# Two steps in turn at each change of resident operands in an encoder layer's projections

## The chip, the cores and the metric

The kernel runs on one core of a Trainium2 chip. Time is device time of the whole program in microseconds (us); lower is better. Before the change it takes 2800.76 us, the median of three runs (2798.44 to 2802.41).

## The reference, cut to what matters

One encoder layer for two requests of 2048 and 1024 tokens (3072 tokens, width 1024), in float32:

```python
z = rmsnorm(x) @ w_in
f = fft2(z[..., :512]).real
zs = gelu(z[..., 512:])
u, v = zs[..., :512], rmsnorm(zs[..., 512:])
g = u * (einsum('hpq,bnqhc->bnphc', w_spatial, v) + b)
x = x + rmsnorm(concat([f, g]) @ w_out)
a = conv3(rmsnorm(x) @ w_up)
gate, up = a[..., :2816], a[..., 2816:]
y = x + rmsnorm((gelu(gate) * up) @ w_down)
...
```

## The kernel before, in words

Each large product, the gating heads' `zs`, the up projection and the down projection, is done by Strassen's scheme: a product of two 2x2 block matrices takes seven block products, numbered B11, B21, T4, T2, T3, T1, B22 (0 to 6), and sums of their results. Each operand is split in two rounded parts, a high part (a cast on ScalarE, L100 and L154) and the rest (a subtraction on VectorE or GpSimd, L101 and L156), and three matmuls replace one. A block product with an inner size of 512 is thus 12 matmuls of 128x512 into one of 8 PSUM banks (`Step.mm`, L200). I call such a block product a **product**, and the seven of one output tile pair a **step**.

A **stage** (`Stage`) keeps one side resident in SBUF: seven operands of four pieces (28 tiles named `sox`, `sow` or `sog`, each made by one ScalarE cast and one subtraction: pieces 0 and 2 on VectorE, 1 and 3 on GpSimd; in the first up block B11 and T2 are all VectorE's). Steps stream past it with their own small operands (`w0u` to `w6u`, names ending in u for up, d for down, g for the gating heads).

The order is: 24 Fourier products in two halves with the 12 gating steps between; 12 mixing steps; three blocks of the up projection (`Up`, three resident sets of tokens, 22 steps each, 7 products of 12 matmuls); three parts of the down projection (`Down`, three resident sets of weights, 12 steps each, the first with 9 matmuls a product). So operands that are resident change five times, twice in `Up`, on entering `Down`, twice in `Down`; the gating heads and the first up block begin with none.

The order of the instructions is written out by hand. `at(slot, order, fn)` puts work into numbered slots; one slot holds one product of TensorE, and within it loads come first, then preparation (PREP), matmuls (MM), what is done with the result (OUT), stores. Each engine runs its instructions in that order and waits by semaphores. SyncE issues all DMAs, in order. A step that begins in slot s prepares `w` of a product two slots ahead (`Step.prep`), then reads the result (`post`): Up keeps four results in PSUM, lets ScalarE scale them (`centre`) and VectorE add the convolution's two other taps to each (`taps`, L1146), and GpSimd multiplies the gate in (`Up.gate`, L1183). In the first up block and in `Down` and the heads, GpSimd also makes four sums of the streamed operand (`Step.sums`, L179 to L182); w4u's subtraction is GpSimd's (`POOL = (4,)`).

At a change of operands `turnover` spreads the 28 pieces of the new stage over ten slots, from six before the first step of the new stage to four after, as the last old step and the first new one run. All large tiles come from one pool `U` of 43 buffers, half-size ones from `H`.

Of the kernel before, what the change touches and what calls it, by code (L numbers as in the profile page):

```python
# [33 lines left out]
def tile_trunk(  # L34
# [8 lines left out]
    H = ctx.enter_context(tc.tile_pool(name="h", bufs=12))  # L43
# [528 lines left out]
    for j, s in ((T4, 9), (T2, 10), (T3, 11), (T1, 12), (B22, 13)):  # L572
        at(s, PREP + 0.6, heads.prep, j)
# [4 lines left out]
    for pr in range(12):  # L578
        s = SB + 7 * pr
        g = Gate(heads, pr)  # L580
        steps(s, g)
# [4 lines left out]
        at(s + 1, OUT + 0.2, g.vout, 0)
        at(s + 5, OUT + 0.2, g.vout, 1)
        at(s + 7, OUT + 0.6, g.vscale)
        at(s + 6, OUT + 0.3, g.uout, 1)
        at(s + 7, OUT + 0.3, g.uout, 0)  # L590
        at(s + 8, OUT + 0.5, g.vnorm, 0)
        at(s + 8, OUT + 0.5, g.vnorm, 1)
        at(s + 10, PREP + 0.5, g.vsplit)
        at(s + 13, MM + 0.5, g.spatial)
        at(s + 13, OUT + 0.5, g.gate)
        at(s + 15, MM + 0.5, g.turn)
        at(s + 15, OUT + 0.5, g.turned)
        at(s + 16, STORE, g.gstore)
# [598 lines left out]
    for blk in range(3):  # L1197
# [5 lines left out]
        if blk:  # L1203
            turnover(s, stage, Up.ORDER)
        else:
            for i, j in enumerate(Up.ORDER):
# [39 lines left out]
    class Down(Step):  # L1246
# [15 lines left out]
        def cstore(self):  # L1262
            for i in range(2):
                for h in range(2):
                    nc.sync.dma_start(c_d[2 * self.tp + i, :, h], self.quads(i)[h])
# [88 lines left out]
    for q in range(3):  # L1354
# [13 lines left out]
        turnover(s, stage)  # L1368
        if q == 2:
            at(s - 2, LOAD, po_load)  # L1370
        for tp in range(12):
            d = Down(stage, q, tp)
            steps(s, d)
            if q == 0:
                at(s + 8, STORE, d.cstore)
                s += 7
                continue
            at(s if d.closing else s + 3, LOAD, d.cload)
            if not d.closing:
                at(s + 6, OUT + 0.2, d.cadd, 1)  # L1380
                at(s + 7, OUT + 0.2, d.cadd, 0)
            if q == 1:
                at(s + 8, STORE, d.cstore2, 1)
                at(s + 9, STORE, d.cstore2, 0)
            elif tp == 11:
                at(s + 1, LOAD, d.closing_load)
                at(s + 2, OUT + 0.1, d.square, 0, 0)
                at(s + 4, OUT + 0.1, d.square, 1, 0)
                at(s + 5, OUT + 0.1, d.square, 1, 1)
                at(s + 6, OUT + 0.1, d.square, 0, 1)  # L1390
                at(s + 6, OUT + 0.2, d.closing_out)
            else:
                e = 3 if d.closing else 0
                at(s + 10 - e, MM, d.squares)
                at(s + 11 - e, LOAD, d.xload)
                at(s + 11 - e, PREP + 0.5, d.scale)
                at(s + 12 - e, PREP + 0.5, d.yout, 1)
                at(s + 14 - e, OUT + 0.3, d.yout, 0)
                at(s + 14 - e, STORE, d.ystore, 1)
# [123 lines left out]
```

## Time and profile before

| | |
|---|---|
| median of three runs | 2800.76 us |
| the profiled execution | 2798.38 us |
| its span on the core | 2796.6 us |
| TensorE busy | 2659.1 us (95%) |
| VectorE busy | 2218.6 us (79%) |
| GpSimd busy | 1361.6 us (49%) |
| ScalarE busy | 1192.7 us (43%) |
| mean clock granted to TensorE | 0.982 |

A busy TensorE is not a TensorE at its peak: matmuls overlap, and in steady steps of `Up` one starts every 0.227 us (19.04 us for the 84 of a step). What is lost is therefore read as the time of a step over 19.04 us, place by place, and the wait that ends last there says why.

### The profile page before, as it was taken

The page shows a single profiled execution, that of the slowest core. Times are in us where ns is not written, and L with a number is a line of the kernel's source. Part 1 is how long each engine was busy: PE and PEld are TensorE (multiplying, and loading weights), DVE is VectorE, ACT ScalarE, POOL GpSimd, SP SyncE. Part 2 cuts the span into 40 slices and gives each one's busy share as a digit, 9 for nine tenths or more (in the row PEclk, how much of TensorE's full clock was granted, in tenths as well). Part 3 has the DMA queues.
Part 4 walks back from the last instruction along what each step waited for, and adds up shares of the span by engine and source line. Part 5 has one row for each costly group of instructions (what it writes and reads, how often), then busy time and mean ns, then how long its engine had stood idle before and what let it go on. Part 6 is the DMA issues. An engine that isn't in the chain of part 4 may idle for free. (4 is left out here: it accounts for less than half of the span.)

```text
span 2796.6 us, 35290 instructions
## 1 busy us (share of the span) xinstructions
PE 2659.1 (95%) x11930; PEld 2173.2 (78%) x11930; DVE 2218.6 (79%) x3295; ACT 1192.7 (43%) x2273; POOL 1361.6 (49%) x867
## 2 busy tenths in 40 slices
PE   8899999998879999989999999999998999999997
PEld 7678887887758888877888877888886877887775
DVE  5788866767888787888777788888888677669998
ACT  5445534564634444454444444444443242214332
POOL 3856612547774656562212233212224347669787
PEclk9999999999989999999999999999999999999999
DMA  9446667567953545464343363334353465466665
GB/s 336 165 154 205 206 229 258 200 198 226 294 210 113 184 162 179 145 215 128 113 133 128 114 225 112 115 124 135 118 176 115 132 218 175 153 201 212 209 210 200
DMA packets 323926, 498.10 MB, mean 178 GB/s; under 512 B 27232, under 2 KB 176224, under 8 KB 323744
## 3 DMA queue, kind: packets, MB, share of 16 engines
q1 hardware_dynamic: 323744, 495.85, 53.7%
q8 instruction: 93, 1.52, 0.2%
q14 instruction: 89, 0.73, 0.1%
HBM read 337.42 MB, written 158.35 MB: 177 GB/s over the span
## 5 line engine op out<-in xcount | busy, mean ns | idle before, releaser
L1183 POOL TENSOR_TENSOR t0u<-t0u,t1u 128x1024 f32<-128x1024 f32 x66 | 184.2, 2791 | 237.3 <-issue 145.1
L101 POOL TENSOR_TENSOR w4u<-a4u,w4u 128x512 fp32r<-128x512 f32 x44 | 57.1, 1297 | 446.2 <-ACT w4u L100 401.9
L200 PE MATMUL p4u<-sox,w4u 128*128 128x512 f32 x792 | 199.3, 399 | 17.0 <-POOL w4u L101 12.2
L200 PE MATMUL p2u<-sox,w2u 128*128 128x512 f32 x792 | 196.6, 397 | 8.2 <-DVE w2u L101 8.2
L200 PE MATMUL p0u<-sox,w0u 128*128 128x512 f32 x792 | 194.1, 393 | 7.9 <-DVE w0u L101 4.8
L200 PE MATMUL p1u<-sox,w1u 128*128 128x512 f32 x792 | 194.3, 394 | 6.8 <-DVE w1u L101 6.8
L200 PE MATMUL p6u<-sox,w6u 128*128 128x512 f32 x792 | 192.8, 392 | 4.0 <-DVE w6u L101 4.0
L200 PEld LDWEIGHTS p4u<-sox,w4u 128*128 128x128 f32 x792 | 150.1, 192 | 56.2 <-POOL w4u L101 17.2
L200 PE MATMUL p3u<-sox,w3u 128*128 128x512 f32 x792 | 191.8, 390 | 1.7 <-DVE w3u L101 1.7
L200 PE MATMUL p5u<-sox,w5u 128*128 128x512 f32 x792 | 191.0, 390 | 1.0 <-DVE w5u L101 1.0
L1134 ACT ACTIVATE t1u<-p2u,cbt,cwt 128x512 f32<-128x512 f32 x66 | 51.4, 779 | 321.3 <-DVE p2u L1122 321.3
L200 PEld LDWEIGHTS p2u<-sox,w2u 128*128 128x128 f32 x792 | 151.3, 192 | 42.2 <-DVE w2u L101 10.5
L200 PEld LDWEIGHTS p0u<-sox,w0u 128*128 128x128 f32 x792 | 149.2, 189 | 42.4 <-DVE w0u L101 7.5
L200 PEld LDWEIGHTS p1u<-sox,w1u 128*128 128x128 f32 x792 | 150.8, 191 | 39.6 <-DVE w1u L101 8.1
L200 PEld LDWEIGHTS p6u<-sox,w6u 128*128 128x128 f32 x792 | 149.7, 189 | 37.0 <-DVE w6u L101 5.7
L200 PEld LDWEIGHTS p3u<-sox,w3u 128*128 128x128 f32 x792 | 148.1, 188 | 33.7 <-DVE w3u L101 3.0
L200 PEld LDWEIGHTS p5u<-sox,w5u 128*128 128x128 f32 x792 | 148.8, 188 | 32.9 <-DVE w5u L101 1.9
L208 ACT COPY ud<-p0d 128x512 f32<-128x512 f32 x34 | 20.0, 587 | 344.7 <-PE p0d L200 344.7
L1134 ACT ACTIVATE t0u<-p1u,cbt,cwt 128x512 f32<-128x512 f32 x66 | 51.4, 779 | 260.7 <-DVE p1u L1128 260.7
L1182 ACT ACTIVATE t0u<-t0u 128x1024 f32<-128x1024 f32 x66 | 70.1, 1062 | 155.4 <-DVE t0u L1146 114.4
L1146 DVE SCALAR_TENSOR_TENSOR t0u<-p6u,cwt,t0u 128x511 f32<-128x511 f32 (+4 forms) x220 | 111.6, 532 | 5.2
L1146 DVE SCALAR_TENSOR_TENSOR t1u<-p2u,cwt,t1u 128x511 f32<-128x511 f32 (+4 forms) x220 | 111.7, 533 | 3.1
(363 smaller groups left out, 7235.5 us busy)
## 6 DMA issues: line engine op xcount, KB each, us to landing
g_d<-t0u SPq DMA_DIRECT2D x66, 512.0 KB, 2.9
srx<-xo_d SPq DMA_DIRECT2D x42, 512.0 KB, 6.8
xT<-xT SPq DMA_DIRECT2D x24, 512.0 KB, 8.5
xc<-xc SPq DMA_DIRECT2D x24, 512.0 KB, 5.7
zz<-z_d SPq DMA_DIRECT2D x48, 256.0 KB, 5.5
xr<-x_po SPq DMA_DIRECT2D x24, 512.0 KB, 5.2
xo_d<-hT SPq DMA_DIRECT2D x48, 256.0 KB, 4.0
ra0d<-g_d SPq DMA_DIRECT2D x24, 512.0 KB, 6.8
```

What stands on the lines that cost most here:

```text
L101: (eng or vec).tensor_tensor(l, src, h.bitcast(F32), op=ALU.subtract)
L200: nc.tensor.matmul(ps, lhsT=w[:, a, k], rhs=op[k][:, b], start=k == 0 and a + b == 0, stop=k == n - 1 and a == 1)
L208: nc.scalar.copy(self.u, p[0])
L1134: nc.scalar.activation(t[:, i], p, AF.Identity, bias=cbt[:, ti : ti + 1], scale=cwt[:, ti, 1:2])
L1146: vec.scalar_tensor_tensor(d, a, w, d, op0=ALU.mult, op1=ALU.add)
L1182: nc.scalar.activation(ga, ga, AF.Gelu_apprx_tanh)
L1183: nc.gpsimd.tensor_tensor(ga, ga, self.t[1], op=ALU.mult)
```

## The change

The two last steps that use a stage and the two first that use the next are run in pairs, product by product: first B11 of the one, then B11 of the other, and so on over 14 slots (`place` and `pos` give a step its first slot and its stride). This is done for the first and last two steps of each up block, the first two of each down part, the last two of the first two parts, and the first two gating steps. `turnover` gets a lead of 12 slots and a span of 22. In the first up block and the heads an operand is prepared every second slot. The sums of paired down steps are made three slots later, `u.POOL` is empty for both of the first up steps, the taps of Up's first half stand at fixed distances from product 4, and `H` has 14 buffers. The loads and sums of the down weights (`wd_load`, `wd_sums`, `wd_store`) move eight slots back. Elsewhere a step of stride 1 keeps its places.

```diff
-    H = ctx.enter_context(tc.tile_pool(name="h", bufs=12))
+    H = ctx.enter_context(tc.tile_pool(name="h", bufs=14))
...
-    def steps(s, step, ahead=2):
-        at(s - 6, LOAD, step.load)
-        at(s - ahead, PREP - 0.2, step.sums)
-        products(s, step)
...
+    def place(s, step, which=None):
+
+        step.s0, step.by = (s, 1) if which is None else (s + which, 2)
+
+    def pos(step, k):
+        return step.s0 + min(k, 0) + step.by * min(max(k, 0), 6) + max(k - 6, 0)
+
+    def steps(step, ahead=2):
+        at(pos(step, -6), LOAD, step.load)
+        at(pos(step, -ahead), PREP - 0.2, step.sums)
+        products(step)
+
+    def products(step):
         for i, j in enumerate(step.ORDER):
-            at(s + i - 2, PREP, step.prep, j)
-            at(s + i, MM, step.mm, j)
-            at(s + i, OUT, step.post, j)
-
-    TURN = 10
-    def turnover(s, stage, order=tuple(range(7))):
+            at(pos(step, i) - 2, PREP, step.prep, j)
+            at(pos(step, i), MM, step.mm, j)
+            at(pos(step, i), OUT, step.post, j)
+
+    def turnover(s, stage, order=tuple(range(7)), lead=6, span=10):
 
         for n in range(28):
             j, k = order[n // 4], n % 4
-            d = s - 6 + n * TURN // 28
+            d = s - lead + n * span // 28
...
-    for j, s in ((T4, 9), (T2, 10), (T3, 11), (T1, 12), (B22, 13)):
+    for j, s in ((T4, 10), (T2, 12), (T3, 14), (T1, 16), (B22, 18)):
         at(s, PREP + 0.6, heads.prep, j)
...
-        steps(s, g)
+        place(*((SB, g, pr) if pr < 2 else (s, g)))
+        steps(g, 0 if pr < 2 else 2)
...
-        at(s + 8, OUT + 0.5, g.vnorm, 0)
-        at(s + 8, OUT + 0.5, g.vnorm, 1)
...
+        at(pos(g, 8), OUT + 0.5, g.vnorm, 0)
+        at(pos(g, 8), OUT + 0.5, g.vnorm, 1)
...
-            turnover(s, stage, Up.ORDER)
+            turnover(s, stage, Up.ORDER, 12, 22)
         else:
             for i, j in enumerate(Up.ORDER):
-                at(s + [-3, -3, -2, -2, -1, 0, 1][i], LOAD, stage.load, j)
-                at(s + [-2, -2, -1, 0, 1, 2, 3][i], PREP - 0.3, stage.prep, j)
+                d = s + max(2 * i - 3, -2)
+                at(d - 1 - (i > 0), LOAD, stage.load, j)
+                at(d, PREP - 0.3, stage.prep, j)
         for ft in range(NFT):
             u = Up(stage, blk, ft)
-            if ft == 0 and blk == 0:
+
+            pair = ft < 2 or ft > NFT - 3
+            place(s - 7 * (ft % 2) if pair else s, u, ft % 2 if pair else None)
+            first = blk == 0 and ft < 2
+            if first:
                 u.POOL = ()
-            if blk == 0 and ft < 2:
-                at(s - (2, 4)[ft], LOAD, u.load)
-                at(s - 2, PREP - 0.2, u.sums)
-                products(s, u)
+                at(u.s0 - 2, LOAD, u.load)
+                at(u.s0 - 2, PREP - 0.2, u.sums)
+                products(u)
...
-            at(s + 4, OUT + 0.1, u.centre, 1)
-            at(s + 5, OUT + 0.2, u.taps, 1, 0)
-            at(s + 6, OUT + 0.1, u.centre, 0)
-            at(s + 6, OUT + 0.2, u.taps, 1, 1)
-            at(s + 7, OUT + 0.2, u.taps, 0, 0)
-            at(s + 8, OUT + 0.6, u.taps, 0, 1)
...
+            at(pos(u, 4), OUT + 0.1, u.centre, 1)
+            at(pos(u, 4) + 1, OUT + 0.2, u.taps, 1, 0)
+            at(pos(u, 4) + 2, OUT + 0.2, u.taps, 1, 1)
+            at(pos(u, 6), OUT + 0.1, u.centre, 0)
+            at(pos(u, 7), OUT + 0.2, u.taps, 0, 0)
+            at(pos(u, 8), OUT + 0.6, u.taps, 0, 1)
...
-        turnover(s, stage)
+        turnover(s, stage, range(7), 12, 22)
...
             d = Down(stage, q, tp)
-            steps(s, d)
+            pair = tp < 2 or tp > 9 and q < 2
+            place(s - 7 * (tp % 2) if pair else s, d, tp % 2 if pair else None)
+            steps(d, -1 if pair else 2)
```

**TensorE, the last two steps of the second up block (`u1_20`, `u1_21`).** In names such as `p0u1_20`, 0 is the product, 1 the block counted from 0, 20 the step. Before, where the first of them ends and the second begins:

```order
L200 MATMUL p1u1_20_14463<-sox112_11143,w1u1_20_14408 128x512 x3
L200 MATMUL p1u1_20_14463<-sox113_11146,w1u1_20_14408 128x512 x3
L200 MATMUL p0u1_21_14493<-sox100_10844,w0u1_21_14434 128x512 x3
L200 MATMUL p0u1_21_14493<-sox101_10847,w0u1_21_14434 128x512 x3
L200 MATMUL p0u1_21_14493<-sox102_10850,w0u1_21_14434 128x512 x3
L200 MATMUL p0u1_21_14493<-sox103_10878,w0u1_21_14434 128x512 x3
L200 MATMUL p3u1_21_14528<-sox130_10881,w3u1_21_14460 128x512 x3
L200 MATMUL p3u1_21_14528<-sox131_10884,w3u1_21_14460 128x512 x3
```

After, at their first products:

```order
L200 MATMUL p0u1_20_14325<-sox100_10711,w0u1_20_14268 128x512 x3
L200 MATMUL p0u1_20_14325<-sox101_10714,w0u1_20_14268 128x512 x3
L200 MATMUL p0u1_20_14325<-sox102_10737,w0u1_20_14268 128x512 x3
L200 MATMUL p0u1_20_14325<-sox103_10760,w0u1_20_14268 128x512 x3
L200 MATMUL p0u1_21_14349<-sox100_10711,w0u1_21_14294 128x512 x3
L200 MATMUL p0u1_21_14349<-sox101_10714,w0u1_21_14294 128x512 x3
L200 MATMUL p0u1_21_14349<-sox102_10737,w0u1_21_14294 128x512 x3
L200 MATMUL p0u1_21_14349<-sox103_10760,w0u1_21_14294 128x512 x3
```

The two steps now read the same resident `sox10*` one right after the other. The last use of B11 (`sox10*`) thus stands twelve products ahead of the end of the stage, where before it stood six ahead.

**VectorE, the taps of the same steps.** Before, from the weight of the second step's first product on:

```order
L101 TENSOR_TENSOR w0u1_21_14434<-a0u1_21_14364,w0u1_21_14434 128x512
L1125 TENSOR_TENSOR p6u1_20_14437<-vu1_20_14358,p6u1_20_14437 128x512
L1146 SCALAR_TENSOR_TENSOR t1u1_20_14425<-p5u1_20_14389,cwt_82,t1u1_20_14425 128x511 x2
L1146 SCALAR_TENSOR_TENSOR t1u1_20_14425<-p5u1_20_14389,cwt_82,t1u1_20_14425 128x1
L1146 SCALAR_TENSOR_TENSOR t1u1_20_14425<-halo_99,cwt_82,t1u1_20_14425 128x1
L101 TENSOR_TENSOR w3u1_21_14460<-a3u1_21_14384,w3u1_21_14460 128x512
L1128 TENSOR_TENSOR p1u1_20_14463<-uu1_20_14334,p1u1_20_14463 128x512
L1146 SCALAR_TENSOR_TENSOR t1u1_20_14425<-p2u1_20_14411,cwt_82,t1u1_20_14425 128x511 x2
L1146 SCALAR_TENSOR_TENSOR t1u1_20_14425<-p2u1_20_14411,cwt_82,t1u1_20_14425 128x1
L1164 SCALAR_TENSOR_TENSOR fix_101<-p2u1_20_14411,cwt_82,part_100 128x1
L1146 SCALAR_TENSOR_TENSOR t0u1_20_14477<-p6u1_20_14437,cwt_82,t0u1_20_14477 128x511 x2
```

After, between products 4 and 6 of the pair (L1153 is the old L1146, L1132 the old L1125):

```order
L1153 SCALAR_TENSOR_TENSOR t1u1_20_14547<-p5u1_20_14485,cwt_82,t1u1_20_14547 128x511 x2
L1153 SCALAR_TENSOR_TENSOR t1u1_20_14547<-p5u1_20_14485,cwt_82,t1u1_20_14547 128x1
L1153 SCALAR_TENSOR_TENSOR t1u1_20_14547<-halo_99,cwt_82,t1u1_20_14547 128x1
L101 TENSOR_TENSOR w1u1_20_14586<-a1u1_20_14500,w1u1_20_14586 128x512
L1132 TENSOR_TENSOR p6u1_20_14592<-vu1_20_14394,p6u1_20_14592 128x512
L1153 SCALAR_TENSOR_TENSOR t1u1_20_14547<-p2u1_20_14533,cwt_82,t1u1_20_14547 128x511 x2
L1153 SCALAR_TENSOR_TENSOR t1u1_20_14547<-p2u1_20_14533,cwt_82,t1u1_20_14547 128x1
L1171 SCALAR_TENSOR_TENSOR fix_101<-p2u1_20_14533,cwt_82,part_100 128x1
L1153 SCALAR_TENSOR_TENSOR t1u1_21_14575<-p5u1_21_14508,cwt_82,t1u1_21_14575 128x511 x2
L1153 SCALAR_TENSOR_TENSOR t1u1_21_14575<-p5u1_21_14508,cwt_82,t1u1_21_14575 128x1
L1153 SCALAR_TENSOR_TENSOR t1u1_21_14575<-halo_99,cwt_82,t1u1_21_14575 128x1
L101 TENSOR_TENSOR w1u1_21_14618<-a1u1_21_14523,w1u1_21_14618 128x512
```

Before, a tap of one step stood between two weight subtractions (L101); now two taps, one of each step, stand there together.

**GpSimd, the first up block.** `s0u` to `s3u` are the sums of a step's streamed operand, es and ds the last mixing step's residual. Before, from the last resident pieces on:

```order
L156 TENSOR_TENSOR sox011_7316<-srx010_7241,sox011_7316 128x512
L156 TENSOR_TENSOR sox013_7322<-srx012_7243,sox013_7322 128x512
L179 TENSOR_TENSOR s0u0_1_7368<-ra1u0_1_7310 128x512
L180 TENSOR_TENSOR s1u0_1_7369<-s0u0_1_7368,ra0u0_1_7309 128x512
L181 TENSOR_TENSOR s2u0_1_7370<-ra0u0_1_7309,ra1u0_1_7310 128x512
L182 TENSOR_TENSOR s3u0_1_7371<-ra0u0_1_7309,s1u0_1_7369 128x512
L93 TENSOR_SCALAR r2111_v_7395<-ss2111_7343 128x2
L94 TENSOR_TENSOR r2111_y_7396<-r2111_v_7395,power_84 128x2
L898 TENSOR_TENSOR es111_7036<-es111_7036,xr1111_7045 128x1024
L898 TENSOR_TENSOR ds111_7100<-ds111_7100,xr1110_7043 128x1024
L101 TENSOR_TENSOR w4u0_1_7427<-s2u0_1_7370,w4u0_1_7427 128x512
```

After, from the sums of the first step on:

```order
L182 TENSOR_TENSOR s3u0_0_7128<-ra0u0_0_7109,s1u0_0_7126 128x512
L179 TENSOR_TENSOR s0u0_1_7158<-ra1u0_1_7143 128x512
L180 TENSOR_TENSOR s1u0_1_7159<-s0u0_1_7158,ra0u0_1_7142 128x512
L181 TENSOR_TENSOR s2u0_1_7160<-ra0u0_1_7142,ra1u0_1_7143 128x512
L182 TENSOR_TENSOR s3u0_1_7161<-ra0u0_1_7142,s1u0_1_7159 128x512
L156 TENSOR_TENSOR sox041_7224<-srx040_7138,sox041_7224 128x512
```

The second step's sums now stand ahead of the resident pieces, and its `w4u` is no longer on GpSimd.

## Rows read from the trace of the kernel before

**Rows 1.** The page: busy time of the engines, share of the span, instructions.
```profile
PE 2659.1 (95%) x11930; PEld 2173.2 (78%) x11930; DVE 2218.6 (79%) x3295; ACT 1192.7 (43%) x2273; POOL 1361.6 (49%) x867
```

**Rows 2.** Windows, TensorE's L200 alone: stretch, length, busy (matmuls), clock, DMA share, GB/s.
```profile
90.75:144.80 54.05, 44.48 (x169) 0.91 0.49 164
778.28:842.35 64.07, 46.84 (x169) 0.84 0.51 183
1215.97:1289.42 73.45, 64.33 (x254) 0.93 0.52 179
1651.17:1705.85 54.68, 43.84 (x170) 0.94 0.52 185
2086.65:2150.86 64.21, 54.59 (x211) 0.92 0.50 157
2279.38:2344.55 65.17, 57.35 (x233) 0.95 0.64 206
2515.91:2581.97 66.06, 59.94 (x254) 0.97 0.64 215
```

**Rows 3.** Windows, steady steps: length, then busy PE, PEld, DVE, ACT, POOL; clock.
```profile
1117.90:1196.79 78.89, 78.01 (x346) 63.62 (x345) 64.44 (x99) 35.94 (x69) 45.16 (x29) 1.00 0.48 156
1460.64:1536.80 76.16, 76.16 (x338) 63.09 (x337) 59.62 (x117) 32.17 (x52) 16.78 (x8) 1.00 0.38 125
1896.11:1972.27 76.16, 76.16 (x338) 63.06 (x337) 64.71 (x133) 32.18 (x52) 16.28 (x8) 1.00 0.39 124
2165.00:2222.12 57.12, 57.12 (x254) 47.30 (x253) 37.52 (x57) 13.92 (x32) 17.68 (x16) 1.00 0.42 129
2382.49:2458.65 76.16, 76.16 (x338) 63.08 (x337) 49.89 (x57) 16.91 (x32) 48.83 (x33) 1.00 0.52 166
2659.96:2740.01 80.05, 78.57 (x338) 62.22 (x337) 76.75 (x73) 26.70 (x48) 64.35 (x41) 1.00 0.67 211
```

**Rows 4.** Timeline, TensorE, second change of blocks: start, length, what, [idle before <-releaser].
```profile
1695.10 4.63 PE L200 MATMUL p2u<-sox,w2u 128*128 128x512 f32 x10 [3.28 <-DVE w2u L101]
```

**Rows 5.** Line L156 on VectorE: operand subtractions, ns min/median/max.
```profile
L156 DVE TENSOR_TENSOR sox<-srx,sox x46: 677/1177/2890, 768.6 to 1698.4; 128x512 fp32r<-128x512 f32 x46
L156 DVE TENSOR_TENSOR sow<-srw,sow x42: 677/1772/2894, 2093.0 to 2556.7; 128x512 fp32r<-128x512 f32 x42
```

**Rows 6.** Timeline, VectorE, the same change of blocks.
```profile
1652.40 0.69 DVE L1128 TENSOR_TENSOR p1u<-uu,p1u 128x512 f32<-128x512 f32 x1
1653.00 1.65 DVE L1146 SCALAR_TENSOR_TENSOR t1u<-p2u,cwt,t1u 128x511 f32<-128x511 f32 x3
...
1659.43 0.68 DVE L1112 TENSOR_TENSOR vu<-uu,p3u 128x512 f32<-128x512 f32 x1
...
1664.70 2.27 DVE L101 TENSOR_TENSOR w6u<-a6u,w6u 128x512 fp32r<-128x512 f32 x1
1666.90 3.47 DVE L156 TENSOR_TENSOR sox<-srx,sox 128x512 fp32r<-128x512 f32 x2
```

**Rows 7.** Timeline, GpSimd, the same change of blocks.
```profile
1657.20 6.43 POOL L156 TENSOR_TENSOR sox<-srx,sox 128x512 fp32r<-128x512 f32 x4 [0.75 <-ACT sox L154]
```

**Rows 8.** Window, VectorE's L156 alone, the same change: length, busy (pieces).
```profile
1640.00:1705.00 65.00, 15.95 (x14) 0.95 0.53 183
```

**Rows 9.** Waits of VectorE over five steps of the second block.
```profile
DVE w0u L101 <- ACT w0u L100: 10.4, 5, 2.1
```

**Rows 10.** Timeline, VectorE, start of the first block.
```profile
768.59 12.56 DVE L156 TENSOR_TENSOR sox<-srx,sox 128x512 fp32r<-128x512 f32 x8
```

**Rows 11.** Timeline, ScalarE, start of the first block.
```profile
777.61 0.62 ACT L100 CAST w0u<-ra0u 128x512 fp32r<-128x512 f32 x1 [7.68 <-DMA ra0u<-w_up]
```

**Rows 12.** Timeline, GpSimd, start of the first block.
```profile
825.65 1.71 POOL L101 TENSOR_TENSOR w4u<-s2u,w4u 128x512 fp32r<-128x512 f32 x1
```

**Rows 13.** Timeline, TensorE, start of the first block.
```profile
827.42 4.18 PE L200 MATMUL p4u<-sox,w4u 128*128 128x512 f32 x10 [7.75 <-POOL w4u L101]
```

**Rows 14.** Timeline, VectorE, gating head of the first step.
```profile
127.36 5.88 DVE L442 SCALAR_TENSOR_TENSOR v2g<-v2g,rvg_y,gsg 128x128 f32<-128x128 f32 x8
```

More of the change, by code (lines that the diff above doesn't have):

```diff
@@ L585, in tile_trunk @@
             at(s - 2, OUT + 0.5, stats[pr].root)
[L586 to L590, printed above, removed]
-        at(s + 8, OUT + 0.5, g.vnorm, 0)
-        at(s + 8, OUT + 0.5, g.vnorm, 1)
[L593 to L598, printed above, removed]
+        at(pos(g, 1), OUT + 0.2, g.vout, 0)
+        at(pos(g, 5), OUT + 0.2, g.vout, 1)
+        at(pos(g, 7), OUT + 0.6, g.vscale)
+        at(pos(g, 6), OUT + 0.3, g.uout, 1)
+        at(pos(g, 7), OUT + 0.3, g.uout, 0)
+        at(pos(g, 8), OUT + 0.5, g.vnorm, 0)
+        at(pos(g, 8), OUT + 0.5, g.vnorm, 1)
+        at(pos(g, 10), PREP + 0.5, g.vsplit)
+        at(pos(g, 13), MM + 0.5, g.spatial)
+        at(pos(g, 13), OUT + 0.5, g.gate)
+        at(pos(g, 15), MM + 0.5, g.turn)
+        at(pos(g, 15), OUT + 0.5, g.turned)
+        at(pos(g, 16), STORE, g.gstore)
     gpm = None
@@ L688, in tile_trunk @@
     for i in range(NFT // 2):
-        at(SB + 7 * i + 1, LOAD, wd_load, i)
-        at(SB + 7 * i + 3, PREP, wd_sums, i)
-        at(SB + 7 * i + 7, STORE, wd_store, i)
+        at(SB + 7 * i + 9, LOAD, wd_load, i)
+        at(SB + 7 * i + 11, PREP, wd_sums, i)
+        at(SB + 7 * i + 15, STORE, wd_store, i)
     class Side:
@@ L1260, in fetch, with cstore @@
                 )
[L1262 to L1265, printed above, removed]
+        def cstore(self, i, h):
+            nc.sync.dma_start(c_d[2 * self.tp + i, :, h], getattr(self, f"c{i + 1}{h + 1}"))
         def cload(self):
@@ L1372, in tile_trunk @@
             d = Down(stage, q, tp)
-            steps(s, d)
+            pair = tp < 2 or tp > 9 and q < 2
+            place(s - 7 * (tp % 2) if pair else s, d, tp % 2 if pair else None)
+            steps(d, -1 if pair else 2)
+            s += 7
             if q == 0:
-                at(s + 8, STORE, d.cstore)
-                s += 7
+                at(pos(d, 2), STORE, d.cstore, 0, 0)
+                at(pos(d, 6), STORE, d.cstore, 1, 0)
+                at(pos(d, 6), STORE, d.cstore, 1, 1)
+                at(pos(d, 7), STORE, d.cstore, 0, 1)
@@ L1377, in tile_trunk @@
                 continue
-            at(s if d.closing else s + 3, LOAD, d.cload)
+            at(pos(d, 0 if d.closing else 3), LOAD, d.cload)
             if not d.closing:
-                at(s + 6, OUT + 0.2, d.cadd, 1)
-                at(s + 7, OUT + 0.2, d.cadd, 0)
+                at(pos(d, 6), OUT + 0.2, d.cadd, 1)
+                at(pos(d, 7), OUT + 0.2, d.cadd, 0)
             if q == 1:
-                at(s + 8, STORE, d.cstore2, 1)
-                at(s + 9, STORE, d.cstore2, 0)
+                at(pos(d, 8), STORE, d.cstore2, 1)
+                at(pos(d, 9), STORE, d.cstore2, 0)
@@ L1385, in tile_trunk @@
             elif tp == 11:
[L1386 to L1391, printed above, removed]
+                at(pos(d, 1), LOAD, d.closing_load)
+                at(pos(d, 2), OUT + 0.1, d.square, 0, 0)
+                at(pos(d, 4), OUT + 0.1, d.square, 1, 0)
@@ L1392, in tile_trunk @@
+                at(pos(d, 5), OUT + 0.1, d.square, 1, 1)
+                at(pos(d, 6), OUT + 0.1, d.square, 0, 1)
+                at(pos(d, 6), OUT + 0.2, d.closing_out)
             else:
                 e = 3 if d.closing else 0
[L1394 to L1399, printed above, removed]
@@ L1400, in tile_trunk @@
-                at(s + 15 - e, STORE, d.ystore, 0)
-            s += 7
+                at(pos(d, 10 - e), MM, d.squares)
+                at(pos(d, 11 - e), LOAD, d.xload)
+                at(pos(d, 11 - e), PREP + 0.5, d.scale)
+                at(pos(d, 12 - e), PREP + 0.5, d.yout, 1)
+                at(pos(d, 14 - e), OUT + 0.3, d.yout, 0)
+                at(pos(d, 14 - e), STORE, d.ystore, 1)
+                at(pos(d, 15 - e), STORE, d.ystore, 0)
     with tc.manual_schedule():
```

13 lines of the change are left out of this document (6 added, 7 removed).

## The prediction

> **What bounds the kernel now.** The page first: TensorE is busy 95% of the span, VectorE 79% [rows 1], but that share counts matmuls that overlap. So I took places one by one, in windows of TensorE's L200 alone [rows 2], against steady steps [rows 3]. A steady step of the second up block takes 76.16/4 = 19.04 us, one of the first down part 57.12/4 = 14.28. What the seven places of the change lose against that:
>
> - first two gating steps: 54.05 - 38.08 = 16.0, of which the first mixing products of the heads, also TensorE work, are a part (about 1.5, an estimate): 14.5
> - first two up steps: 64.07 - 38.08 = 26.0
> - up block 0 to 1: 73.45 - 57.12 = 16.3
> - up 1 to 2: 54.68 - 38.08 = 16.6
> - up to down: 64.21 - 19.04 - 28.56 = 16.6
> - down 0 to 1: 65.17 - 14.28 - 38.08 = 12.8
> - down 1 to 2: 66.06 - 57.12 = 8.9
>
> Together 111.7 us, 4% of the span. No change of order can give more.
>
> Which engine is late there? The timeline of up 1 to 2: a steady product takes 19.04/7 = 2.72 us, and in the change TensorE stops in the middle of products, waiting for a weight that VectorE has yet to subtract, 3.28 us in one case, after which ten matmuls alone took 4.63 [rows 4]; the mean clock granted over that window was 0.94 [rows 2]. VectorE is in order and full: besides its own work it makes 14 of the 28 pieces. Alone one takes 0.68 us (the least), but the median is 1.18 in up and 1.77 in down [rows 5]: it stretches while GpSimd makes the other pieces beside it. Two took 3.47 and a weight subtraction 2.27, while a sum that reads PSUM took 0.68 within GpSimd's four pieces [rows 6, 7]. So **VectorE bounds the changes, and GpSimd lengthens its work**. The 14 pieces took 15.95 us there [rows 8]; with the 2 x 1.6 by which two weights were stretched, about 19 us of extra VectorE work. Ten slots have about 2 us free for it and the weights stand about 1.5 us ahead: 19 - 2 - 1.5 = 15.5, near the 16.6 seen.
>
> **The change, part by part.**
>
> *More slots.* Free VectorE time per step is its idle time less one wait for ScalarE's cast behind `centre`, 10.4/5 = 2.1 us, which does not go away [rows 9]. From rows 3: second up block (76.16 - 59.62)/4 - 2.1 = 2.0; first (78.89 - 64.44)/4 - 2.1 = 1.5; third (76.16 - 64.71)/4 - 2.1 = 0.8; down 0, with about 1.5 kept for the like wait, 3.4; down 1, 5.1; down 2, whose steps already take 20.0, under 1. Six slots more on each side are 6/7 step of each: 3.0, 2.4, 3.6, 7.3 and 5.0 us for the five changes, 21 in all. These are savings if nothing else moves.
>
> *Fewer meetings with GpSimd.* With 1.3 pieces a slot where there were 2.8, a subtraction meets GpSimd less often. If none did, 14 pieces would cost 14 x 0.68 = 9.5 and not 16, and the weights 3 less: up to 9.6 us per change. If all still do, nothing. I take a third to a half.
>
> *Two steps' taps together.* This costs. In the pair the late work of both up steps falls between its slots 9 and 15. There VectorE has, at a spacing of 0.6 us per full operation and 1.65 per tap, 1.8 with its small end [rows 6], seven weights (4.2), seven sums (4.2), eight taps (14), two waits behind `centre` (4.3) and four or five pieces (2.7): 29.4 us, against seven slots of 2.72 (19.0) and the two slots by which a weight is prepared ahead (5.4). In the light slots before, it cannot run ahead, since the sums wait for TensorE. So a last pair loses 5 us in this count, and with some four subtractions stretched by about 0.8, 8. A first pair has one or two pieces in that stretch: about 5. Taps are shorter in block 0 (two long instructions for three) and 0.3 us longer each in block 2 (VectorE 64.71 against 59.62 in four steps [rows 3]).
>
> That makes: up 0 to 1, 6.3 + 5 = 11.3, for 16.3, saves 5 (1 to 9). Up 1 to 2, 8 + 6.5 = 14.5, saves 2 (loses 1, saves 5). Up to down, 10.5 for the last pair and 2.5 for the light down pair: 13, saves 3.5 (0 to 6.5). Down 0 to 1 has no taps; VectorE's load per slot (a weight, a sum, 0.64 pieces) stays at about its length: 4 lost for 12.8, saves 9 (5 to 11).
>
> *Down 1 to 2* would lose 3 for 8.9, but the third part needs buffers: 28 resident tiles, the gain, four c and four x1 tiles of the pair, four split weights and the streamed pairs come to over 43 units of `U`, so ScalarE's square into x1 and the casts behind it wait for TensorE's products. I put that at 4.5 us (0 to 9): no row of before shows it; its steps' excess, (80.05/4 - 19.04) = 1.0 per step over four or five steps, is nearest. Saves 1.5 (loses 5, saves 5).
>
> *First up block.* VectorE made eight pieces in 12.56 us ahead of the first weight [rows 10], which itself waited for its load 7.68 us, until 777.61 [rows 11]. Now four pieces come ahead of it and its load stands ahead of four others in SyncE's queue. The second step's w4u, which waited in GpSimd's queue until 825.65 behind the residual [rows 12] and stopped TensorE for 7.75 us [rows 13], goes to VectorE: +0.6 to 1.7 there, with two slots of lead. Per pair of slots VectorE then has two to four pieces, two weights and two sums, 5 to 7 us for 5.44. Following the order with these durations the pair ends some 9 us earlier. The bounds: the w4u stop alone, less some 4.5 for taps and meetings (3), and that stop with half of the 12.56, less 2 (12).
>
> *Gating steps.* Preparing every second slot helps up to 5, but the norms of both steps (5.88 each [rows 14]) now follow in two slots, behind which the third step's weights queue: 11.8 for 5.4. I take 0 (-5 to 5).
>
> *No cost*: the down weights' sums, four GpSimd operations a step (6.43/4 = 1.6 each [rows 7], so 6.4 if they came on the path), stay beside TensorE's gating steps. A change's 14 loads stand six slots earlier in SyncE's queue, ahead of streamed operands; DMA is 0.50 to 0.64 busy there [rows 2], and old tiles come free at two a slot where 1.3 are asked for, so I count nothing; a load that is late would cost what one was late at the start of up, up to 7.68 [rows 11]. Two more `H` buffers can only take waits away. Single steps keep their order.
>
> Sum: 9 + 5 + 2 + 3.5 + 9 + 1.5 + 0 = **30 us** saved, from 2798.4 of the profiled execution to 2768.4; that one lies 2.4 below the median, so I predict 2770.8 for the median.
>
> **The rivals.** A measurement here tells about 0.2% (5.6 us) from no change.
>
> - *Forecast*: 18 to 42 saved, 2759 to 2783; chance 0.55.
> - *Meetings vanish*: spread pieces find GpSimd free nearly always. Another 5 us at each of the five changes, 2.5 to 5 at each start: 55 to 65 saved at best, 43 at least; 2736 to 2758. For it: the 0.68 minimum. Against: ScalarE casts pieces for both engines one after the other, so they still start together. 0.12.
> - *Meetings stay*: every piece still meets one. Then 15 less than forecast or more: 6 to 18 saved, 2783 to 2795. For it: the median of 1.77 in down, where GpSimd has sums of its own. 0.16. The Trainium skill, SBUF — State Buffer, section "Who interferes with whom", states that a VectorE instruction with two SBUF inputs and a GpSimd instruction that reads SBUF exclude each other for the whole instruction; by this rule the total of exclusion is not reduced by spreading, only its chance of meeting, and the time would be this rival's. The trace agrees with the rule's first half (3.47 for two against 0.68 for the sum from PSUM).
> - *Nothing gained*: VectorE's work is the same and only moves; 2795 to 2806. 0.07.
> - *Slower*: taps of both steps in one place, six up pairs. It decides if a pair loses over 12: that is if about all 12 subtractions in the crowded slots are stretched to 1.7 (+12). Six pairs at 15 are 90 us, for 75.5 now lost at those four places, and the two norms add up to 8 in the heads: 15 + 8 - 9 of down 0 to 1 = +14: 2815. Against: GpSimd is busy under half of those slots. 0.10.
>
> **How the numbers follow.** Faster by over 0.2%: 0.55 + 0.12 + 0.16 = 0.83; within 0.07; slower 0.10. The range 2750 to 2794 leaves out the slower case, most of no change and the better half of the vanished meetings, 0.2.
>
> **What would show it.** In the changed profile, the same windows over two pairs: up to 11 us lost on each side of an up change; 4 at down 0 to 1; the first two up steps losing 17. VectorE's L156 median near 1.0 in up. In the late slots of up's pairs TensorE is stopped for w1u, w0u and w3u, 0.5 to 2 us each time. I am wrong if a change of the up blocks loses as much as before with VectorE idle in it (a load, a buffer or ScalarE is then late), if the down changes still lose over 8, or if steps away from the pairs take other than 19.04.

## The result: slower by 0.9%, and the profile after

The changed kernel takes 2826.62 us, the median of five runs (2815.22 to 2836.0), beside 2800.76 for the kernel before on the same chip (2798.44 to 2806.46): a ratio of 1.0093, 95% interval 1.0077 to 1.0110. I had forecast 2770.8. The profiled execution is the longest of the five, 2836.0 us with a span of 2834.2, so its losses are somewhat larger than those of the median. Its page:

```profile
PE 2675.3 (94%) x11930; PEld 2178.2 (77%) x11930; DVE 2244.9 (79%) x3296; ACT 1197.2 (42%) x2273; POOL 1347.4 (48%) x866
```

TensorE's busy time grew by 16.2 us and VectorE's by 26.3 with no work added [rows 1]; so instructions got longer. To see where, I cut both spans at the same steps. The windows of TensorE's L200 in the kernel before; columns: stretch, length, matmuls, weight loads, clock, DMA share, GB/s. In order they are the first three gating steps, six single gating steps (the 5th to 10th), the first four up steps, six steps over up 0 to 1, six over up 1 to 2, six over up to down, four over down 0 to 1, four over down 1 to 2 and the four behind these:

```profile
90.75:167.87 77.12, 64.33 (x253) 49.55 (x252) 0.93 0.48 161
190.95:329.86 138.91, 118.83 (x505) 93.33 (x506) 1.00 0.59 196
778.28:880.43 102.15, 84.92 (x337) 67.32 (x337) 0.90 0.47 165
1196.93:1327.50 130.57, 121.45 (x506) 97.37 (x505) 0.96 0.50 167
1632.13:1762.97 130.84, 120.00 (x506) 95.85 (x504) 0.97 0.51 165
2067.61:2179.42 111.81, 102.19 (x421) 80.87 (x420) 0.95 0.48 151
2265.10:2344.55 79.45, 71.63 (x296) 56.95 (x294) 0.96 0.68 222
2496.87:2581.97 85.10, 78.98 (x338) 63.89 (x336) 0.98 0.68 229
2581.97:2660.10 78.13, 77.66 (x337) 62.45 (x336) 1.00 0.67 215
```

The same steps in the changed kernel:

```profile
86.59:156.39 69.80, 61.33 (x253) 47.61 (x252) 0.98 0.27 88
178.70:358.73 180.03, 132.15 (x505) 103.13 (x505) 0.90 0.47 155
818.27:923.19 104.92, 86.53 (x337) 66.50 (x336) 0.92 0.48 170
1239.08:1366.38 127.30, 120.06 (x505) 92.88 (x504) 1.00 0.50 165
1671.02:1800.65 129.63, 119.93 (x505) 93.04 (x504) 1.00 0.50 165
2105.29:2215.61 110.32, 100.96 (x421) 80.29 (x420) 0.97 0.45 147
2301.29:2371.19 69.90, 68.11 (x295) 54.80 (x294) 1.00 0.68 221
2523.51:2607.67 84.16, 79.11 (x337) 63.81 (x336) 0.98 0.66 219
2607.67:2698.32 90.65, 82.28 (x338) 65.53 (x336) 0.94 0.55 185
```

Line by line, before less after: +7.3, **-41.1**, -2.8, +3.3, +1.2, +1.5, +9.6, +0.9, **-12.5**; together -32.6 of the 37.6 us by which the two spans differ, and of the rest the eleventh gating step alone took 7.6 more. The changes of operands inside the two projections gained, as wanted; the loss lies in the gating steps that are *not* paired and run one after the other as before, 23.2 us each before and 30.0 now, and in the third down part, one or two steps behind its pair.

**A single gating step.** The timeline of the changed kernel, VectorE, then GpSimd, then TensorE (L448 is the old L442):

```profile
247.05 10.27 DVE L448 SCALAR_TENSOR_TENSOR v2g<-v2g,rvg_y,gsg 128x128 f32<-128x128 f32 x8
257.24 0.68 DVE L101 TENSOR_TENSOR w4g<-s2g,w4g 128x512 fp32r<-128x512 f32 x1
...
246.61 1.30 POOL L126 TENSOR_TENSOR wt<-wd,wd 128x512 f32<-128x512 f32 x1 [6.08 <-DMA wd<-wd]
...
255.87 1.31 POOL L182 TENSOR_TENSOR s3g<-ra0g,s1g 128x512 f32<-128x512 f32 x1
...
257.98 4.63 PE L200 MATMUL p4g<-sog,w4g 128*128 128x512 f32 x10 [5.66 <-DVE w4g L101]
```

The same place before:

```profile
221.47 5.62 DVE L442 SCALAR_TENSOR_TENSOR v2g<-v2g,rvg_y,gsg 128x128 f32<-128x128 f32 x8
...
220.64 1.29 POOL L130 TENSOR_TENSOR wd<-wd,wd 128x512 f32<-128x512 f32 x1
```

Eight short norms stand ahead of `w4g` on VectorE. Now eight GpSimd operations, the four sums of the down weights (L126 to L130) and the step's own four (L179 to L182), 1.3 us each and back to back, begin just as the norms do (0.44 us ahead), because GpSimd waited 6.08 us for the down weights' load, which the change issues one slot later within a step. Each norm waits for one of them: 10.27/8 = 1.28 us. Before, the last of the four down-weight sums (L130) began 0.83 us ahead of the norms, and only it and the three behind it lay beside them. `w4g` is then late, TensorE stops 5.66 us, and the next ten matmuls take 4.63 us where ten behind a stop of 0.76 took 2.56 (a row further down): about half the rate. In that stretch, 257.98 to 262.60, the granted clock was 0.50, the lower of its two levels (1.2 GHz). The groups by line, all 96 norms, ns least/median/most, before and after:

```profile
L442 DVE SCALAR_TENSOR_TENSOR v2g<-v2g,rvg_y,gsg x96: 334/344/1447, 127.4 to 391.1; 128x128 f32<-128x128 f32 x96
```

```profile
L448 DVE SCALAR_TENSOR_TENSOR v2g<-v2g,rvg_y,gsg x96: 335/1345/1455, 135.9 to 430.0; 128x128 f32<-128x128 f32 x96
```

And TensorE's waits over the six steps (us in total, times, longest), before and after:

```profile
PE p4g L200 <- DVE w4g L101: 5.0, 6, 1.3
```

```profile
PE p4g L200 <- DVE w4g L101: 32.8, 6, 6.0
```

27.8 us more of waiting and six times about 2.1 for the slow ten make 40, of the 41.1 lost. The Trainium skill, SBUF — State Buffer, section "Who interferes with whom", says that a VectorE operation with two SBUF inputs and a GpSimd operation that reads SBUF keep each other out for the whole instruction. For VectorE these rows agree, 1.28 us a norm against 1.30 a sum; GpSimd is not seen to wait here, its sums take 1.3 us also where no norm is beside them (in the run e7 below).

**The start of the up projection.** VectorE, GpSimd and TensorE there, after:

```profile
814.05 7.36 DVE L156 TENSOR_TENSOR sox<-srx,sox 128x512 fp32r<-128x512 f32 x3
...
824.20 6.84 DVE L156 TENSOR_TENSOR sox<-srx,sox 128x512 fp32r<-128x512 f32 x4
...
854.50 5.63 DVE L156 TENSOR_TENSOR sox<-srx,sox 128x512 fp32r<-128x512 f32 x2
...
819.16 1.71 POOL L179 TENSOR_TENSOR s0u<-ra1u 128x512 f32<-128x512 f32 x1
...
830.46 1.70 POOL L182 TENSOR_TENSOR s3u<-ra0u,s1u 128x512 f32<-128x512 f32 x1
...
853.47 3.37 POOL L905 TENSOR_TENSOR es<-es,xr 128x1024 f32<-128x1024 f32 x1 [3.84 <-DVE es L904]
...
832.76 4.46 PE L200 MATMUL p0u<-sox,w0u 128*128 128x512 f32 x10 [5.02 <-DVE w0u L101]
...
861.85 4.64 PE L200 MATMUL p2u<-sox,w2u 128*128 128x512 f32 x10 [5.09 <-DVE w2u L101]
```

The old stop of 7.75 us for `w4u` [rows 13] is gone, but both steps' sums, eight in a row, and then the residual stand beside VectorE's resident pieces (seven pieces 14.2 us, two pieces 5.63), and TensorE now stops 5.02 us for the second `w0u` and 5.09 for `w2u`.

**The third down part.** ScalarE, VectorE and TensorE, after, in and just ahead of its fourth step, which took 30.99 us where it had taken 19.19:

```profile
2618.75 1.06 ACT L1322 ACTIVATE x10d<-c0d 128x1024 f32<-128x1024 f32 x1 [1.52 <-PE p3d L200]
...
2641.51 3.37 DVE L1357 SCALAR_TENSOR_TENSOR c0d<-c0d,r4d_y,gpo 128x1024 f32<-128x1024 f32 x1
2644.80 0.68 DVE L101 TENSOR_TENSOR w3d<-s1d,w3d 128x512 fp32r<-128x512 f32 x1
...
2633.27 4.63 PE L200 MATMUL p1d<-sow,w1d 128*128 128x512 f32 x10 [3.08 <-DVE w1d L101]
...
2645.53 4.14 PE L200 MATMUL p3d<-sow,w3d 128*128 128x512 f32 x10 [3.80 <-DVE w3d L101]
...
2667.24 2.56 PE L200 MATMUL p3d<-sow,w3d 128*128 128x512 f32 x10 [0.76 <-DVE w3d L101]
```

ScalarE's squares and casts wait for TensorE's products, as foreseen, and then, as I read these rows, the pair's outputs come late and together with those of the next step: VectorE's weights `w1d` and `w3d` queue behind them.

### The profile page after: what moved, and what is told of

The parts are those of the page before. It is cut to its first block, busy times and chain, and to the rows that moved or that the text cites. A ratio compares the mean times of both kernels' runs of the same rounds, so it can differ in the third digit from the quotient of the medians.

```text
span 2834.2 us, 35131 instructions
## 1 busy us (share of the span) xinstructions
PE 2675.3 (94%) x11930; PEld 2178.2 (77%) x11930; DVE 2244.9 (79%) x3296; ACT 1197.2 (42%) x2273; POOL 1347.4 (48%) x866
## 5 line engine op out<-in xcount | busy, mean ns | idle before, releaser
L101 POOL TENSOR_TENSOR w4u<-a4u,w4u 128x512 fp32r<-128x512 f32 x44 | 59.1, 1342 | 411.5 <-ACT w4u L100 411.5
L200 PE MATMUL p0u<-sox,w0u 128*128 128x512 f32 x792 | 197.2, 397 | 11.7 <-DVE w0u L101 11.1
L200 PE MATMUL p1u<-sox,w1u 128*128 128x512 f32 x792 | 194.3, 394 | 10.4 <-DVE w1u L101 10.2
L200 PE MATMUL p4u<-sox,w4u 128*128 128x512 f32 x792 | 193.8, 393 | 6.7 <-POOL w4u L101 6.3
L200 PE MATMUL p3u<-sox,w3u 128*128 128x512 f32 x792 | 192.6, 392 | 5.7 <-DVE w3u L101 4.2
L200 PE MATMUL p2u<-sox,w2u 128*128 128x512 f32 x792 | 192.2, 393 | 6.1 <-DVE w2u L101 6.1
L200 PE MATMUL p6u<-sox,w6u 128*128 128x512 f32 x792 | 190.7, 390 | 0.3 <-DVE w6u L101 0.2
L200 PE MATMUL p5u<-sox,w5u 128*128 128x512 f32 x792 | 189.9, 389 | 0.2
L200 PEld LDWEIGHTS p0u<-sox,w0u 128*128 128x128 f32 x792 | 149.9, 191 | 49.0 <-DVE w0u L101 16.6
L200 PEld LDWEIGHTS p1u<-sox,w1u 128*128 128x128 f32 x792 | 148.5, 189 | 46.5 <-DVE w1u L101 14.8
L200 PEld LDWEIGHTS p4u<-sox,w4u 128*128 128x128 f32 x792 | 146.8, 188 | 45.5 <-POOL w4u L101 11.2
L200 PEld LDWEIGHTS p2u<-sox,w2u 128*128 128x128 f32 x792 | 149.8, 190 | 38.4 <-DVE w2u L101 7.3
L200 PEld LDWEIGHTS p3u<-sox,w3u 128*128 128x128 f32 x792 | 147.4, 188 | 41.2 <-DVE w3u L101 7.4
L200 PEld LDWEIGHTS p6u<-sox,w6u 128*128 128x128 f32 x792 | 149.1, 189 | 32.4 <-DVE w6u L101 1.4
L200 PEld LDWEIGHTS p5u<-sox,w5u 128*128 128x128 f32 x792 | 148.5, 188 | 31.9 <-DVE w5u L101 1.1
L1153 DVE SCALAR_TENSOR_TENSOR t0u<-p6u,cwt,t0u 128x511 f32<-128x511 f32 (+4 forms) x220 | 111.6, 532 | 5.1 <-ACT halo L1143 0.2
L1153 DVE SCALAR_TENSOR_TENSOR t1u<-p2u,cwt,t1u 128x511 f32<-128x511 f32 (+4 forms) x220 | 111.7, 533 | 3.1
```

Of the source, the lines that this page charges most:

```text
L101: (eng or vec).tensor_tensor(l, src, h.bitcast(F32), op=ALU.subtract)
L200: nc.tensor.matmul(ps, lhsT=w[:, a, k], rhs=op[k][:, b], start=k == 0 and a + b == 0, stop=k == n - 1 and a == 1)
L1153: vec.scalar_tensor_tensor(d, a, w, d, op0=ALU.mult, op1=ALU.add)
```

## The experiments

Each ratio is to the kernel before, timed beside the run on the same chip (2798.9 to 2800.8 us), with its 95% interval.

**The down weights one slot earlier** (e1), seven slots behind their old place instead of eight, in the changed kernel. (All eight slots undone there was not tried.)

```diff
-        at(SB + 7 * i + 9, LOAD, wd_load, i)
-        at(SB + 7 * i + 11, PREP, wd_sums, i)
-        at(SB + 7 * i + 15, STORE, wd_store, i)
+        at(SB + 7 * i + 8, LOAD, wd_load, i)
+        at(SB + 7 * i + 10, PREP, wd_sums, i)
+        at(SB + 7 * i + 14, STORE, wd_store, i)
```

> The changed kernel with the down weights' loads, sums and stores moved back by seven slots (a whole step) and not eight, so that they have the place within a gating step that they had before. Theory A (in steps 4 to 10 of the gating heads GpSimd's eight sums, four of the down weights and four of the step, run while VectorE does the eight short norms of the gate, L448, and each norm waits for one of them; the eighth slot made them meet): those steps go from about 30 us back to about 23, the eight norms from 10.3 us to about 6, and the time from 2826 to 2770-2790. Theory B (the steps are late for another reason: streamed operands issued late because SyncE waits for w4g's buffers, or the pair at the start): the steps stay near 30 us and the time stays over 2815.

2798.38 us, ratio 1.000 (0.9991 to 1.0009): between the two theories, in the range of neither. One slot takes 28 us off, so the place of these four operations costs, but norms still take 6.2 to 6.7 us and a step 24.2.

**Only this delay, in the kernel before** (e2): the slots 9, 11 and 15 as in the change, nothing else.

> The kernel before with only the down weights' loads, sums and stores moved by eight slots; nothing else changed. Theory A: ten or so gating steps go from 23 to about 30 us, so 2800 becomes 2845-2875. Theory B (pairs, 14 half buffers or late streamed operands are needed for it): gating steps stay at 23 us, 2798-2806.

2798.47 us, ratio 1.000 (0.999 to 1.001). Theory A in this form falls: the later place alone costs nothing, it needs something else of the change.

**The sums two slots later still** (e3), in the changed kernel: load, sums and store at 9, 13 and 17.

> The changed kernel with loads of the down weights where the change put them (slot 9) but their four GpSimd sums two slots later (13) and the stores at 17, so that they stand behind the step's own sums on GpSimd. Theory A: only four sums in a row meet the norms at most; norms at 6 us or under, gating steps at 22 to 25 us, time 2770-2800. Theory B (lateness of what SyncE loads): unchanged loads, so steps near 30 us and over 2815. A mixture (the sums meet something else): between.

2778.86 us, ratio 0.9926 (0.9913 to 0.9940): faster than both kernels. Norms take 3.3 us with one GpSimd operation beside them, a gating step 21.4 to 22.3.

**The third down part's first two steps one after the other** (e4), in the changed kernel:

```diff
-            pair = tp < 2 or tp > 9 and q < 2
+            pair = q < 2 and (tp < 2 or tp > 9)
...
-        turnover(s, stage, range(7), 12, 22)
+        turnover(s, stage, range(7), 12, 16 if q == 2 else 22)
```

> The changed kernel with the first two steps of the third down part run one after the other again (the last two steps of the second part stay paired; the new operands are spread over 16 slots, from 12 before to 4 after). Theory A (the pair's eight c and x1 buffers run out of pool U and both steps' outputs come together; 11.8 us lost in the fourth step): 8 to 13 us less than the changed kernel, the fourth step at 19 to 20 us and not 31. Rival (the fourth step waits for its loads or for DMA): within 3 us of the changed kernel.

2812.62 us, ratio 1.0049 (1.0035 to 1.0064), and the fourth step is back at 19.21. So that pair's loss is its own, 11.8 us in that step. The 14 us between the medians need not all be this pair's: the gating steps, untouched here, took 219 us from the fourth to the eleventh in this profile where the changed kernel's took 233: two of its steps had norms of 4.3 and 6.5 us. The same code falls into the bad meeting in some steps and not in others.

**Both repairs** (e5): e3 and e4 together.

> The changed kernel with two of its parts altered together: the down weights' sums two slots later (as in e3) and the third down part's first two steps one after the other (as in e4). Theory A (two separate causes: GpSimd's eight operations in a row beside the eight norms in the single gating steps; buffers of U in the first pair of the third part): the savings add, 2778.9 - 12 = 2767 us (2761 to 2772), gating steps 4 to 10 at 21.4 to 22.3 each, the fourth step of the third part at 19.2. Rival (both losses are one late stream that comes back somewhere): 2775 or more, with the difference at another place.

2762.69 us (2762.28 to 2766.14), ratio 0.9866 (0.9851 to 0.9881): the savings add. This profile's windows, six single gating steps, the first four up steps, the third part's pair, and the four steps behind it:

```profile
174.56:306.59 132.03, 116.98 (x504) 93.80 (x505) 1.00 0.62 207
756.90:861.26 104.36, 86.50 (x337) 66.26 (x336) 0.92 0.48 170
2502.47:2545.87 43.40, 39.85 (x169) 31.07 (x168) 1.00 0.52 170
2545.87:2624.00 78.13, 76.96 (x337) 62.69 (x336) 1.00 0.67 215
```

**And the first up block's first pair undone** (e6), on top of e5:

```diff
-                d = s + max(2 * i - 3, -2)
-                at(d - 1 - (i > 0), LOAD, stage.load, j)
-                at(d, PREP - 0.3, stage.prep, j)
+                at(s + [-3, -3, -2, -2, -1, 0, 1][i], LOAD, stage.load, j)
+                at(s + [-2, -2, -1, 0, 1, 2, 3][i], PREP - 0.3, stage.prep, j)
...
-            pair = ft < 2 or ft > NFT - 3
+            pair = blk > 0 and ft < 2 or ft > NFT - 3
...
-                at(u.s0 - 2, LOAD, u.load)
+                at(s - (2, 4)[ft], LOAD, u.load)
```

> As e5, with the first two steps of the first up block one after the other again (their old loads, sums and order of preparation), but w4u of the second step left on VectorE. Theory P (in the pair GpSimd's eight sums of both steps stand in a row beside VectorE's seven resident pieces, about 2 us each, and the residual beside the next two; one step at a time this does not happen and the old stop of 7.75 us for w4u is gone): the four steps from the start take 95 to 99 us where they take 104.5, and the time is 5 to 9 below e5. Rival Q (VectorE's pieces meet GpSimd's work in either order): 101 to 104 us there, the time within 3 of e5.

2761.91 us (2760.28 to 2765.39): 0.8 below e5, within the spread. The four steps took 99.3 us where e5's took 104.4, just above what theory P said; the time as a whole is what rival Q said. In this profile the work ahead of them took 5.9 more (3.0 of it ahead of the gating heads) and down 0 to 1 1.9 more. VectorE's eight first pieces cost 12.55 us again, as before [rows 10]. At this place pairing loses about 5 us against moving `w4u` alone in these two profiles; in the whole time it does not show.

**The sums away from the norms, in the kernel before** (e7): slots 9, 13, 17 in place of 1, 3, 7.

> The kernel before, with the loads, sums and stores of the down weights at slots 9, 13 and 17 in place of 1, 3 and 7 of a gating step. Theory A (what a gating step loses is set by how many GpSimd operations stand beside its eight norms; the sums now stand away from them): single gating steps at 21.4 to 22.3 us where they took 23.1, norms at 3 to 4 us where they took 5.2 to 5.9, the time 2780 to 2788. Rival D (the gain of e3 needs the paired steps or the two further H buffers): gating steps at 23, 2796 to 2801.

2793.38 us, ratio 0.998 (0.9969 to 0.9991). The gating steps did what theory A says: no GpSimd operation stands beside the norms, they take 2.2 us and six steps 132.03. But only 7 us arrive: from the twelfth gating step to the up projection 434.8 us passed where 425.4 had. There a Fourier product behind the heads waits 5.2 us for the cast of its streamed operand, where the longest such wait had been 0.4. My range missed that, and what makes the operand late was not tried.

**The kernel before, the delay of the change, and 14 buffers in H** (e8), which is e2 with one number altered:

```diff
-    H = ctx.enter_context(tc.tile_pool(name="h", bufs=12))
+    H = ctx.enter_context(tc.tile_pool(name="h", bufs=14))
```

> The kernel before with the down weights eight slots back as in the change (9, 11, 15) and H at 14 buffers: e2 had 12 and lost nothing. Theory E (two more buffers let the loads run so far ahead that sums and norms fall together): single gating steps at 27 to 30 us, 2835 to 2860. Rival F (it takes the first two steps in turn to set it off): gating steps at 23, 2796 to 2801.

2844.6 us (2841.65 to 2855.84), ratio 1.0152 (1.0134 to 1.0170): worse than the change itself, without any paired step. The windows of six single gating steps in e8, e2, e3 and e7:

```profile
200.07:376.88 176.81, 131.94 (x505) 102.91 (x505) 0.90 0.47 153
```

```profile
186.74:326.73 139.99, 120.17 (x504) 94.43 (x505) 0.99 0.61 195
```

```profile
176.66:308.65 131.99, 116.96 (x504) 93.77 (x505) 1.00 0.62 207
```

```profile
182.55:314.58 132.03, 116.98 (x504) 93.80 (x505) 1.00 0.64 208
```

Norms and first down-weight sum in one step of e8, then in one of e2:

```profile
265.94 10.72 DVE L442 SCALAR_TENSOR_TENSOR v2g<-v2g,rvg_y,gsg 128x128 f32<-128x128 f32 x8
...
265.98 1.29 POOL L126 TENSOR_TENSOR wt<-wd,wd 128x512 f32<-128x512 f32 x1 [6.56 <-DMA wd<-wd]
```

```profile
239.23 3.22 DVE L442 SCALAR_TENSOR_TENSOR v2g<-v2g,rvg_y,gsg 128x128 f32<-128x128 f32 x8
...
240.42 1.36 POOL L126 TENSOR_TENSOR wt<-wd,wd 128x512 f32<-128x512 f32 x1 [3.94 <-DMA wd<-wd]
```

The order on every engine is the same in both. With 12 buffers the sums come 1.19 us behind the first norm; five norms slip through, the sixth waits for the first sum, and the last two pass while GpSimd waits 0.66 us for its next load. With 14 the sums come 0.04 us behind the first norm, and all eight are caught. What theory E forecast came out; by which waits two more buffers move the sums was not followed.

**H back to 12 in the changed kernel** (e9), that one number alone:

> The changed kernel with one number undone: H has 12 buffers again. Theory E (the two further buffers are what tips the gating steps, as they did in the old kernel with the down weights eight slots back): single gating steps fall from 30 to 22 to 23.5 us, about 48 us less than the changed kernel, 2770 to 2785. Rival F (in the changed kernel the paired steps tip them whatever H has): gating steps at 28 to 30, 2810 or more.

2783.31 us (2778.93 to 2792.99), ratio 0.9942 (0.9926 to 0.9957): 43 us gone for one number. So without the two buffers the change is 17 us faster than the kernel before, in spite of its loss in the third down part. Single gating steps take 23.3 us on average, and norms 2.2 to 5.4 us in all but one (8.57):

```profile
176.17:315.94 139.77, 119.68 (x504) 94.36 (x505) 0.99 0.63 199
```

**One buffer more in U for the third part's pair** (e10): e3 with H 12 and U 44.

> As e3 (down weights' sums two slots later), with the two buffers of H given to U: H 12, U 44. Theory U (in the first pair of the third down part ScalarE's square and the casts behind it wait for a buffer of U that a product of TensorE still holds): one buffer more takes away the first of the three waits, the fourth step of that part falls from 30.99 to 22 to 28 us, gating steps stay at 21.4 to 22.3: 2768 to 2776. Rival V (there the two steps' outputs meet on VectorE and GpSimd, buffers or not): the step stays at 30 to 31, 2775 to 2782.

2780.49 us (2778.35 to 2782.13), no gain on e3. The fourth step fell from 30.99 to 28.12, so buffers seem to be a part of it, just short of what theory U said (`H` was altered too); the time is in rival V's range, and the rest may be the meeting of outputs that it names. Other places took the gain back (3 us more in the first three gating steps). How the loss divides stays open.

## Why the prediction was wrong

**The step that failed** stands under "No cost": "Two more `H` buffers can only take waits away", and beside it that the down weights' sums "stay beside TensorE's gating steps" at no cost. The first sentence took every wait for a loss, and the second looked only at whether TensorE has other work meanwhile. With 12 buffers GpSimd's eight operations start behind VectorE's first norms; with 14, and with the sums at their later place, they start with them or ahead, and the norms ahead of `w4g` went from 5.2 to 5.6 us a step to 8.3 to 10.3: 41 us over six steps and 48 over the eight from the fourth to the eleventh. e2 and e8 differ in that number alone, by 46 us; the changed kernel and e9 also, by 43. I had the mechanism in hand, VectorE's two-input operations stretched by GpSimd's [rows 5 to 7], and applied it to the resident pieces only. [Rows 14] already showed norms of 5.88 us, which at their least of 0.334 each need under 3: that row should have been read as "four meetings", and the move of the four sums priced by it: up to eight meetings instead of four, about 5 us a step, in all the steps that have these sums. That would have been the price of the bad case only: e2 moves the sums too and loses nothing.

**"Single steps keep their order"** is true of the order and wrong as an argument: times shifted, not order. The sixteen middle steps of the second and the third up block do take 304.64/16 = 19.04 as before, and those of the first 19.7 as before. But my sign of being wrong, steps away from the pairs that take other than before, came true in the third down part too: its fourth step takes 30.99.

**Down 1 to 2**: the running out of `U` was put at 4.5 us. The two stretches lost 0.9 - 12.5 = -11.6 us against before where I had +1.5; the wait on buffers is seen, but the term was mis-sized: e4 gives 11.8 us back in the fourth step alone, outside my 0 to 9. That late outputs meet those of the next step is a reading of the rows; e10 takes only 2.9 us of it away with one buffer more.

**First up steps**: +9 forecast, -2.8 measured. The stop for `w4u` went, as I said; what I left out is that the second step's sums, moved ahead, stand beside VectorE's pieces (the order showed it). e6 gets to 99.3 us there without the pair, though it does not part the sums from the rest of the pair: the term was an argument for moving `w4u`, not for pairing.

**Right, or nearly**: down 0 to 1 saves 9.6 (9 forecast), its four steps lose 69.90 - 14.28 x 2 - 38.08 = 3.3 (4). Up 0 to 1 +3.3 (5), up 1 to 2 +1.2 (2), up to down +1.5 (3.5), each within its bounds and below its middle. A likely reason shows in the groups of L156, after:

```profile
L156 DVE TENSOR_TENSOR sox<-srx,sox x46: 678/1196/2892, 811.2 to 1742.3; 128x512 fp32r<-128x512 f32 x46
L156 DVE TENSOR_TENSOR sow<-srw,sow x42: 678/1636/1790, 2114.4 to 2595.7; 128x512 fp32r<-128x512 f32 x42
```

The medians, 1.20 and 1.64 against 1.18 and 1.77 [rows 5], hardly moved, where I had named 1.0 in up as a sign: pieces seem to meet GpSimd about as often as before. That is the premise of the rival "meetings stay", and the pairs' places fit it: all windows but the six single gating steps add up to 8.5 us saved, in that rival's 6 to 18. That is partly luck: the sum holds the 12.5 us lost in the third part, and +7.3 from the three steps with the gating pair, which I had put at 0 (-5 to 5). The kernel is slower, but not as my "slower" rival had it, by bunched taps: in the two changes inside Up TensorE's longest stop for a weight was 1.7 and 2.7 us, where I had forecast 0.5 to 2.

**The sum as forecast, 30 us, needed two repairs**: with the sums away from the norms and the third part's pair undone (e5) the kernel is 37.7 us faster than the one before, some 7 of it in single gating steps, which now take 22.0 us where they had taken 23.2.

## What to carry to other kernels

When operations move, look not only for what covers them but for what runs beside them on the engine that they keep waiting: count GpSimd operations beside each run of short VectorE operations, and price every meeting at up to a whole GpSimd operation. A wait that disappears also shifts what starts when, so a bigger pool is a change of schedule and has to be measured alone. Where a step repeats, look at several: the same code met GpSimd in some gating steps and not in others.

## What was not expected of the hardware

A VectorE norm of 0.335 us beside a row of GpSimd operations of 1.3 us takes as long as one of these: eight cost 10.3 to 10.7 us in the steps shown instead of 2.2 (e7, none beside), while the GpSimd operations keep their 1.3. It can go the other way: in the step of e2 ahead of the one shown, a down-weight sum that began 1.01 us behind the first norm took 3.53 us, and the eight norms kept their 2.18.

Which of the two it is goes largely by the start. I compare the six single gating steps of the changed kernel and of e8 with those of e2 and e9, by the first GpSimd sum that lies beside the norms. With 14 buffers it begins between 0.93 us ahead of the first norm and 0.04 behind it in eleven of twelve steps, and the norms take 8.3 to 10.7 us in ten of these (6.05 in one; 7.52 in the twelfth, with 0.63 behind). With 12 it begins 0.24 to 1.50 us behind, and the norms take 2.2 to 6.4 us in eleven (8.57 where it was 0.24). The lead does not settle it alone: in e2 the norms take 2.18 us with 1.01 of it, and 4.33 with 1.32.

Why 12 buffers hold the sums just that far back, and why the bad meeting then comes back step after step, was not shown by a run. I suppose that a late `w4g` makes the loads behind it on SyncE late, and these the next sums. It fits that from 190 to 380 us SyncE waited 52.3 us for `w4g`'s subtraction in the changed kernel and 20.0 in e2.
